# Seven-product MLP of a two-layer encoder: tiles on multiples of 512 bytes, and both layers' ends in another order

## The chip, the cores and the metric

The kernel runs on one core of a Trainium2 chip. The metric is device time in microseconds; runs of the kernel before gave 1194.27, 1194.92 and 1196.45 us, median 1194.92. Engines of a core: TensorE (PE, with its weight loads, PEld), VectorE (DVE), ScalarE (ACT), GpSimd (POOL) and SyncE (SP, whose queue issues most transfers). Each runs its own instructions in order; semaphores tie them together.

## What is computed

Two layers of an encoder on x of 512 tokens by 1024, everything in float32: attention (half stick-breaking heads, half differential heads) with an output projection, then an MLP with squared ReLU, each behind an RMSNorm and added to x, and one RMSNorm at the end.

```python
for l in range(DEPTH):                                   # DEPTH = 2
    h = rmsnorm(x, attn_norm[l])
    proj = jnp.einsum('bsd,de->bse', h, w_in[l])         # 1024 -> 3072
    ...
    x = x + jnp.einsum('bse,ed->bsd', mixed, w_o[l])
    h = rmsnorm(x, mlp_norm[l])
    u = jnp.square(jax.nn.relu(jnp.einsum('bsd,df->bsf', h, w_ff1[l])))   # D_FF = 4096
    x = x + jnp.einsum('bsf,fd->bsd', u, w_ff2[l])
return rmsnorm(x, final_norm)
```

## The kernel before

**Numbers.** Every fp32 operand of a large product is held as two parts: hi, a rounded copy made by ACT (L116 for weights, L223 for u), and lo, the rest, made by DVE (L117, L224). A product is three matmuls, hi with hi, hi with lo, lo with hi (`three`, L280 to L282), each 128 x 128 by 512 columns. The hi and lo parts of a weight unit (128 x 1024) take turns in four slots in the MLP: two in pool `wspl`, which lives through the whole kernel, and two in pool `f2`, opened for each layer's MLP. In attention only the first two are used.

**State.** x is kept transposed: eight tiles of 128 features by 512 tokens. h is x times the norm's gain, in hi and lo. The RMS factor of the MLP's input is not multiplied into h; since relu squared is homogeneous of degree two, its square (r2, one column for each 128 tokens, `column(tb)`) scales the output of the MLP.

**Attention.** `dense` yields the projections, matmul block by matmul block; `attn` yields the pieces of the heads' work. A loop interleaves them: for each cost of dense work, `credit` grows by cost * (ATT - spent) / (DENSE - TAIL - done), and attention pieces are issued while credit lasts. ATT = 54, DENSE = 145, TAIL = 6. What is left of attention at the end of dense follows in one go. In layer 1 the first two projection blocks (16 units of three matmuls) have already run at the end of layer 0 (`opened_by`).

**MLP.** Four groups of 1024 hidden features. Each has eight up-projection blocks (f, 24 matmuls each: weights stationary, h moving, L280 to L282). `evict_u` makes u in tile F (relu and square on ACT) and from it the sums and differences for a seven-product scheme (after Strassen) over halves of tokens and halves of features, split into Ah and Al. Then come seven forms in the order of FORMS, 24 matmuls each: Ah or Al stationary, the weight slot moving.

```python
FORMS = ("11", "21", "x1", "22", "x2", "x3", "x4")
```

The weight operands of forms 11, 21 and 22 are loaded as they are (`fetch`, SP's queue); those of x1, x2, x4 and x3 arise in place from accumulating transfers on POOL's queue (`grow`, L788). Products gather in seven tiles y (two banks of 128 tokens by 512 features each, `gather`, L838 to L840).

**Ends of the layers.** In the last group, the seven sums are combined to the four quarters of the output: `merge` (L848) adds one y to another by an accumulating transfer on POOL's queue, `join` (L845) does it on DVE. `settle` scales by column(tb): on ACT (L866), or on DVE as a scalar_tensor_tensor out of PSUM (L857). Layer 0 then transposes back into x (`back`: four transposes yT on PE, L871, an add on DVE, L872, and a new h), and starts the next layer's first projections, p. Layer 1 instead transposes x (xT, L862, inside `settle`) and adds it to y (L863), squares on ACT with a running sum (L881), `root` takes the power -1/2 on POOL (L886 to L889), `weigh` multiplies by the final gains, which lie in cos_t and sin_t (L893), and `store` scales and sends a half row out (L900 to L904). Banks for xT and yT have the tag "t", of which there are two.

**What sets the order.** Within an engine, the order is that of the program as the build's scheduler lays it out; PE, DVE, ACT and the queues of POOL and SP each hold to it. A tile's address follows from the order and sizes of tiles in the pools: cp (x, h, constants, up to the filler `trail`), wraw, wspl, and then the pool fp of the layer with y, kept (q), r2, F, Ah, Al and, in layer 1, four tiles `sum`; last comes f2.

## Time and profile before

| | |
|---|---|
| median of three runs | 1194.92 us |
| the profiled execution's own time | 1193.42 us |
| its span, first to last instruction | 1191.7 us |
| mean granted TensorE clock | 0.996 |
| layer 0: attention up to about 260, MLP about 260 to 580 us | |
| layer 1: attention about 580 to 860, MLP about 860 to 1181, end of the layer to 1191.7 | |

The profile is one execution. A row of a group reads: line, engine, operation, tile written <- tiles read, shapes, count | busy time, mean duration of one | idle time ahead of it on its engine, with what released it. A row in order of time reads: start, duration (of all merged ones together), engine, line, operation, tiles, count, and in brackets the idle time just before it and who ended it. Names of tiles come without their numbers; y tiles of the x forms are merged as yx, those of 11, 21 and 22 as y, and the PSUM banks of forms are 21030 (form 21, layer 0, group 3, bank 0) or x. Matmul rows overlap, so the distance from one start to the next is the measure of PE's pace.

### The profile page before, as it was taken

The numbers are of one execution on the slowest core, as the hardware profiler recorded it, in microseconds if no ns is written. First come the engines' busy times: TensorE is split into PE (matmuls) and PEld (weight loads), VectorE is DVE, ScalarE is ACT, GpSimd is POOL, SyncE is SP. The second block draws the span as 40 slices with busy tenths as digits, with TensorE's granted clock in tenths as the row PEclk, the third lists the DMA queues.
The fourth block names the chain that finished last, engine by engine and source line by source line (L and its number), as shares of the span: only waits on it lengthen the run. The fifth ranks groups of instructions, "written<-read, shape, count | busy, mean of one in ns | idle before, by whom it ended". The sixth has DMA issues, their size and how long they took to land.

```text
span 1191.7 us, 15321 instructions
## 1 busy us (share of the span) xinstructions
PE 1161.9 (98%) x5454; PEld 952.5 (80%) x5454; DVE 820.7 (69%) x1307; ACT 650.7 (55%) x1147; POOL 216.3 (18%) x281
## 2 busy tenths in 40 slices
PE   9999999999999999999999899999999999999995
PEld 6887888888888888888777788888888888888884
DVE  7888788765546646555978777887764466575668
ACT  6455666566655455455535455665665553653643
POOL 1221543120101001001011225332110010010021
PEclk9999999999999999999999999999999999999999
DMA  7545334254835837637326544432558367375273
GB/s 241 171 137 168 125 106 124 72 212 115 221 124 122 219 102 155 199 90 157 89 87 173 137 153 124 132 98 71 218 126 216 112 134 219 89 175 178 36 157 109
DMA packets 56716, 169.58 MB, mean 142 GB/s; under 512 B 7104, under 2 KB 8128, under 8 KB 56640
## 3 DMA queue, kind: packets, MB, share of 16 engines
q1 hardware_dynamic: 46416, 131.88, 33.7%
q0 software_dynamic: 10080, 36.70, 17.6%
q8 instruction: 43, 0.70, 0.2%
q14 instruction: 33, 0.27, 0.1%
q10 hardware_dynamic: 144, 0.02, 0.0%
HBM read 138.17 MB, written 2.10 MB: 118 GB/s over the span
## 4 chain that ended last, share of the span: by engine, by line
PE 80%; DVE 6%; DMA 4%; issue 4%; ACT 2%; POOL 2%; SPq 0%; POOLq 0%; DVEq 0%; ACTq 0%
PE f L281 10%; PE f L280 10%; PE f L282 10%; PE x L280 4%; PE x L281 4%; PE x L282 4%; DMA q<-in_w 2%; PE wo L280 2%; PE wo L281 2%; PE wo L282 2%; DVE wlo L117 1%; ACT whi L116 1%; PE T0s L554 1%; PE T1s L554 1%; DMA kl1d2k<-hl1d2k 1%
## 5 line engine op out<-in xcount | busy, mean ns | idle before, releaser
L117 DVE TENSOR_TENSOR wlo<-raw,whi 128x1024 fp32r<-128x1024 f32 (+1 forms) x132 | 158.9, 1207 | 105.0 <-ACT whi L116 104.3
L117 DVE TENSOR_TENSOR wlo<-q,whi 128x512 fp32r<-128x512 f32 x224 | 146.0, 686 | 98.1 <-ACT whi L116 98.0
L281 PE MATMUL f<-h_lo,whi 128*128 128x512 f32 x512 | 201.4, 393 | 0.0
L116 ACT ACTIVATE whi<-raw 128x1024 fp32r<-128x1024 f32 (+1 forms) x132 | 133.9, 1020 | 123.4 <-PE f L281 60.3
L280 PE MATMUL f<-h_hi,whi 128*128 128x512 f32 x512 | 201.0, 393 | 0.0
L282 PE MATMUL f<-h_hi,wlo 128*128 128x512 f32 x512 | 200.6, 392 | 0.0
L116 ACT ACTIVATE whi<-q 128x512 fp32r<-128x512 f32 x224 | 129.8, 625 | 127.3 <-PE f L281 38.0
L788 POOL DMA_DIRECT2D q<-in_w x64 | 55.9, 877 | 570.1 <-DVE wlo L117 493.4
L280 PEld LDWEIGHTS f<-h_hi,whi 128*128 128x128 f32 x512 | 96.1, 188 | 22.1
L282 PEld LDWEIGHTS f<-h_hi,wlo 128*128 128x128 f32 x512 | 96.1, 188 | 21.7
L281 PEld LDWEIGHTS f<-h_lo,whi 128*128 128x128 f32 x512 | 96.1, 188 | 21.5
L224 DVE TENSOR_TENSOR Al<-F,Ah 128x256 fp32r<-128x256 f32 (+2 forms) x96 | 74.8, 779 | 44.7 <-ACT Ah L223 44.7
L280 PE MATMUL x<-whi,Ah 128*128 128x512 f32 x256 | 101.8, 398 | 0.0
L281 PE MATMUL x<-wlo,Ah 128*128 128x512 f32 x256 | 101.4, 396 | 0.0
L282 PE MATMUL x<-whi,Al 128*128 128x512 f32 x256 | 101.1, 395 | 0.0
L223 ACT ACTIVATE Ah<-F 128x256 fp32r<-128x256 f32 (+2 forms) x96 | 67.6, 704 | 45.0 <-DVE F L824 43.0
L282 PEld LDWEIGHTS x<-whi,Al 128*128 128x128 f32 x256 | 48.4, 189 | 11.3
L280 PEld LDWEIGHTS x<-whi,Ah 128*128 128x128 f32 x256 | 48.4, 189 | 11.2
L281 PEld LDWEIGHTS x<-wlo,Ah 128*128 128x128 f32 x256 | 48.4, 189 | 11.0
L815 ACT ACTIVATE F<-f 128x512 f32<-128x512 f32 x64 | 37.6, 588 | 8.1 <-PE f L282 4.4
L816 ACT ACTIVATE F<-F 128x512 f32<-128x512 f32 x64 | 40.3, 630 | 1.5
L485 POOL TENSOR_TENSOR sig1s<-sig1s,C1s 128x128 f32<-128x128 f32 (+3 forms) x32 | 25.9, 809 | 61.9 <-DVE C1s L482 30.7
(1051 smaller groups left out, 2572.7 us busy)
## 6 DMA issues: line engine op xcount, KB each, us to landing
raw<-in_w SPq DMA_DIRECT2D x126, 512.0 KB, 3.5
q<-in_w SPq DMA_DIRECT2D x64, 512.0 KB, 5.5
q<-in_w POOLq DMA_DIRECT2D x64, 512.0 KB, 5.6
x<-in_xT SPq DMA_DIRECT2D x8, 256.0 KB, 4.3
raw<-in_w SPq DMA_DIRECT2D x8, 128.0 KB, 4.3
yx<-y POOLq DMA_DIRECT2D x2, 512.0 KB, 7.4
y<-y POOLq DMA_DIRECT2D x2, 512.0 KB, 8.1
y<-yx POOLq DMA_DIRECT2D x2, 512.0 KB, 6.2
```

Source lines behind the costliest of these rows:

```text
L116: h = nc.scalar.activation(hi[:, a:b], raw[:, a:b], AF.Copy)
L117: self.last = h, nc.vector.tensor_tensor(out=lo[:, a:b], in0=raw[:, a:b], in1=hi[:, a:b].bitcast(F32), op=ALU.subtract)
L223: nc.scalar.activation(hi, src, AF.Copy)
L224: nc.vector.tensor_tensor(out=lo, in0=src, in1=hi.bitcast(F32), op=ALU.subtract)
L280: nc.tensor.matmul(pt, ah, bh, start=first, stop=False)
L281: nc.tensor.matmul(pt, ah, bl, start=False, stop=False)
L282: nc.tensor.matmul(pt, al, bh, start=False, stop=last)
L485: nc.gpsimd.tensor_mul(sig[:, 0:wd], sig[:, 0:wd], C[:, 1 : wd + 1])
L554: nc.tensor.transpose(pt[:, off : off + P], u["w"][qi][:, kb * P : (kb + 1) * P], ident)
L788: nc.gpsimd.dma_start(t, quad(g, q, c), accum_op=ALU.add)
L815: nc.scalar.activation(t, pt, AF.Relu)
L816: nc.scalar.activation(t, t, AF.Square)
```

## The change

1. r2 and the sums leave fp: a tile `fin` of 24 columns in cp holds them, taken out of the filler `trail`, so that no other address in cp changes. What stands behind them in fp and f2 moves: F, Ah, Al and both f2 slots start on multiples of 512 bytes.
2. In layer 1, `done` starts at 2 * KC * 3 * 0.216 = 10.37, the cost of the two projection blocks that layer 0 has run.
3. The loads of cos_t and sin_t are issued in group 1 of the MLP; in layer 1, ACT scales both by the square root of D in group 2 (sin_t with a minus), and `weigh` and `root` lose those factors.
4. In the last group, merge 21 <- 11 follows gather 21 in place of gather 11.
5. Layer 0's end: y's rows are scaled by r2 on ACT beforehand, where they are complete, and products from PSUM or from x3 are multiplied and added (`add_to`). The join x4 <- x3 goes. Transposes back start after six of eight products of x4, in pairs, and the next layer's first products go in the order of c. All squares stand behind the last h.
6. Layer 1's end: for tokens 0 to 255, the second half gathers in "z", two quads' tiles that start as minus the transposed x (ACT) and get x1 times r2 by a transfer; two joins go; rows 2 and 3 are settled, squared and weighed within x3, and stored in the middle of x4.

```diff
     clo = cp.tile([P, 4], F32, tag="clo", name="clo")
     ones_r = cp.tile([P, 1], F32R, tag="onesr", name="ones_r")
     nc.vector.memset(ones_r.bitcast(F32), 1.0)
-    cp.tile([P, 112], F32, tag="trail", name="trail")
+    fin = cp.tile([P, 24], F32, tag="fin", name="fin")
+    cp.tile([P, 88], F32, tag="trail", name="trail")
 
...
             at = attn()
-            done = spent = credit = 0.0
+            done = 2 * KC * 3 * 0.216 if l else 0.0
+            spent = credit = 0.0
             live = True
...
             y = {f: fp.tile([P, 2, 512], F32, tag="y" + f, name=f"y{f}_{l}") for f in FORMS}
-            if not last:
-                nc.sync.dma_start(cos_t, cos)
-                nc.sync.dma_start(sin_t, sin)
-            else:
-                nc.sync.dma_start(cos_t, gfin[0:512].partition_broadcast(P))
-                nc.sync.dma_start(sin_t, gfin[512:1024].partition_broadcast(P))
-
             def quad(g, q, c):
...
             fresh = set(FORMS)
-            home = {(1, 0): "21", (1, 1): "22", (0, 0): "x4", (0, 1): "x1"}
+            home = {(1, 0): "21", (1, 1): "22", (0, 0): "x4", (0, 1): "z" if last else "x1"}
 
...
 
-            def settle(tb, j, banks_=None):
+            def turned(tb, j):
+                pt = bank("t", f"xT{tb}{j}")
+                for k in range(4):
+                    nc.tensor.transpose(pt[:, k * P : (k + 1) * P], x[:, 4 * j + k, tb * P : (tb + 1) * P], ident)
+                return pt
+
+            def settle(tb, j):
                 o = place(tb, j)
-                if banks_:
+                if last:
                     nc.vector.scalar_tensor_tensor(
-                        out=o, in0=banks_[tb % 2], scalar=column(tb), in1=o, op0=ALU.mult, op1=ALU.add)
-                elif last:
-                    pt = bank("t", f"xT{tb}{j}")
-                    for k in range(4):
-                        nc.tensor.transpose(pt[:, k * P : (k + 1) * P], x[:, 4 * j + k, tb * P : (tb + 1) * P], ident)
-                    nc.vector.scalar_tensor_tensor(
-                        out=o, in0=o, scalar=column(tb), in1=pt, op0=ALU.mult, op1=ALU.subtract if j else ALU.add)
+                        out=o, in0=o, scalar=column(tb), in1=turned(tb, j), op0=ALU.mult,
+                        op1=ALU.subtract if j else ALU.add)
                 else:
                     nc.scalar.activation(o, o, AF.Copy, scale=column(tb))
+
+            def add_to(tb, j, src):
+                o = place(tb, j)
+                nc.vector.scalar_tensor_tensor(
+                    out=o, in0=src, scalar=column(tb), in1=o, op0=ALU.mult, op1=ALU.add)
 
...
 
-            sums = {}
-
             def square(tb, j):
-                if tb not in sums:
-                    sums[tb] = fp.tile([P, 4], F32, tag=f"sum{tb}", name=f"sum{tb}")
                 nc.scalar.activation(
-                    ft(f"junk{tb}{j}"), place(tb, j), AF.Square, accum_out=sums[tb][:, j : j + 1])
+                    ft(f"junk{tb}{j}"), place(tb, j), AF.Square, accum_out=fin[:, 4 * tb + 4 + j : 4 * tb + 5 + j])
 
             def root(tb):
-                m = sums[tb]
-                nc.vector.tensor_tensor(out=m[:, 2:3], in0=m[:, 0:1], in1=m[:, 1:2], op=ALU.add)
-                nc.vector.tensor_scalar(
-                    out=m[:, 2:3], in0=m[:, 2:3], scalar1=1.0 / D, scalar2=EPS, op0=ALU.mult, op1=ALU.add)
-                nc.gpsimd.tensor_tensor(out=m[:, 3:4], in0=m[:, 2:3], in1=mhalf[:, 0:1], op=ALU.pow)
+                m = [fin[:, 4 * tb + 4 + n : 4 * tb + 5 + n] for n in range(4)]
+                nc.vector.tensor_scalar(out=m[2], in0=m[0], scalar1=m[1], scalar2=D * EPS, op0=ALU.add, op1=ALU.add)
+                nc.gpsimd.tensor_tensor(out=m[3], in0=m[2], in1=mhalf[:, 0:1], op=ALU.pow)
 
             def weigh(tb, j):
                 o = place(tb, j)
-                nc.vector.scalar_tensor_tensor(
-                    out=o, in0=o, scalar=-1.0 if j else 1.0, in1=(cos_t, sin_t)[j], op0=ALU.mult, op1=ALU.mult)
+                nc.vector.tensor_mul(o, o, (cos_t, sin_t)[j])
 
             def store(tb, j, weighed):
                 o = place(tb, j)
-                r = sums[tb][:, 3:4]
+                r = fin[:, 4 * tb + 7 : 4 * tb + 8]
                 if weighed:
...
 
-            r2 = fp.tile([P, 4], F32, tag="r2", name=f"r2{l}")
+            r2 = fin[:, 0:4]
             for g in range(GROUPS):
                 forms = {}
+                end = g == GROUPS - 1
+                if g == 1:
+                    if not last:
+                        nc.sync.dma_start(cos_t, cos)
+                        nc.sync.dma_start(sin_t, sin)
+                    else:
+                        nc.sync.dma_start(cos_t, gfin[0:512].partition_broadcast(P))
+                        nc.sync.dma_start(sin_t, gfin[512:1024].partition_broadcast(P))
+                if g == 2 and last:
+                    nc.scalar.activation(cos_t, cos_t, AF.Copy, scale=math.sqrt(D))
+                    nc.scalar.activation(sin_t, sin_t, AF.Copy, scale=-math.sqrt(D))
                 for k in range(2 * GP):
...
                     evict_u(pt, g, k, forms)
-                end = g == GROUPS - 1
+                    if end and k in (2, 3):
+                        settle(k - 2, 0)
                 for f, form in enumerate(FORMS):
...
                               n == mine[0], n == mine[-1])
-                        if tail and n == len(work) // 2 - 1:
-                            if last:
-                                settle(0, 0, to)
-                                square(0, 0)
-                                root(0)
-                                store(0, 0, False)
-                                store(0, 1, True)
-                            else:
-                                for c_ in CAME[:4]:
-                                    back(c_)
+                        if end and last and form == "x3" and n == 3:
+                            join("22", "x2")
+                            for tb in (2, 3):
+                                settle(tb, 1)
+                                square(tb, 1)
+                                root(tb)
+                                weigh(tb, 0)
+                        if tail and last and n == 3:
+                            add_to(0, 0, to[0])
+                            square(0, 0)
+                            weigh(2, 1)
+                            weigh(3, 1)
+                            root(0)
+                            for tb in (2, 3):
+                                for j in range(2):
+                                    store(tb, j, True)
+                        if tail and not last and n == 5:
+                            for c_ in CAME[:2]:
+                                back(c_)
                     if tail:
                         break
-                    if end and form == "x3":
+                    if end and not last and form == "x3":
                         for tb in (0, 1):
-                            settle(tb, 1, to)
+                            add_to(tb, 1, to[tb])
                     gather(form, to)
...
                         merge("x2", "11")
+                    elif form == "21":
                         merge("21", "11")
...
                             settle(tb, 0)
-                    elif form == "x2":
-                        join("x3", "x2")
-                        join("x1", "x3")
-                        join("22", "x2")
-                        for tb in (0, 1, 2, 3):
-                            settle(tb, 1)
                         if last:
                             for tb in (2, 3):
                                 square(tb, 0)
-                                square(tb, 1)
-                                root(tb)
+                            y["z"], t = (e.rearrange("p (a t) -> p a t", a=2) for e in kept[2])
+                            for tb in (0, 1):
+                                nc.scalar.activation(place(tb, 1), turned(tb, 1), AF.Copy, scale=-1.0)
+                                nc.scalar.activation(t[:, tb, :], y["x1"][:, tb, :], AF.Copy, scale=column(tb))
+                            y["t"] = t
+                            merge("z", "t")
+                    elif form == "x2":
+                        join("x3", "x2")
+                        if not last:
+                            join("x1", "x3")
+                            join("22", "x2")
+                            for tb in range(4):
+                                settle(tb, 1)
                     elif form == "x3":
-                        join("x4", "x3")
-                        for tb in (0, 1):
-                            settle(tb, 0)
                         if last:
                             for tb in (0, 1):
+                                add_to(tb, 1, y["x3"][:, tb, :])
                                 square(tb, 1)
-                                weigh(tb, 1)
-                            for tb in (2, 3):
-                                for j in range(2):
-                                    weigh(tb, j)
-                                    store(tb, j, True)
+                        for tb in (0, 1):
+                            add_to(tb, 0, y["x3"][:, tb, :])
             if last:
-                settle(1, 0, to)
+                add_to(1, 0, to[1])
                 square(1, 0)
+                store(0, 0, False)
+                weigh(0, 1)
+                store(0, 1, True)
+                weigh(1, 1)
                 root(1)
...
                 for tb in (0, 1):
-                    settle(tb, 0, to)
-                squares = []
-                for n, c in enumerate(CAME[:4]):
-                    squares.append(add_sq(c, n == 0, ft, nc.vector))
-                for i in range(2):
-                    for n, c in enumerate(CAME[:4]):
-                        three(pts[i], wpair(us[i], c), hpair(c), n == 0, False)
-                        if i == 1 and n in (1, 3):
-                            for c_ in CAME[4:6] if n == 1 else CAME[6:]:
-                                h = back(c_)
-                for c in CAME[4:]:
+                    add_to(tb, 0, to[tb])
+                for c in CAME[2:4]:
+                    back(c)
+                for n, c in enumerate(CAME):
+                    if n in (2, 3):
+                        for c_ in (CAME[4:6], CAME[6:])[n - 2]:
+                            h = back(c_)
                     for i in range(2):
-                        three(pts[i], wpair(us[i], c), hpair(c), False, c == CAME[-1])
-                for c in CAME[4:]:
-                    squares.append(add_sq(c, False, ft, nc.vector))
-                behind(squares[4][0], h[0])
-                behind(squares[4][1], h[1])
+                        three(pts[i], wpair(us[i], c), hpair(c), n == 0, c == CAME[-1])
+                squares = [add_sq(c, n == 0, ft, nc.vector) for n, c in enumerate(CAME)]
+                for n in (0, 1):
+                    behind(squares[n][n], h[n])
+                for p, q in zip(squares[1:], squares):
+                    behind(p[0], q[0])
                 opened_by.append(pts)
 
 
```

## The prediction

> **What bounds the kernel now.** I read the page first: busy shares, the engines of the chain that ended last, and the two dearest kinds of matmul.
>
> ```profile
> PE 1161.9 (98%) x5454; PEld 952.5 (80%) x5454; DVE 820.7 (69%) x1307; ACT 650.7 (55%) x1147; POOL 216.3 (18%) x281
> ...
> PE 80%; DVE 6%; DMA 4%; issue 4%; ACT 2%; POOL 2%; SPq 0%; POOLq 0%; DVEq 0%; ACTq 0%
> ...
> L280 PE MATMUL f<-h_hi,whi 128*128 128x512 f32 x512 | 201.0, 393 | 0.0
> ...
> L280 PE MATMUL x<-whi,Ah 128*128 128x512 f32 x256 | 101.8, 398 | 0.0
> ```
>
> PE is busy for 98% of the 1191.7 us span. A matmul row lasts 393 to 398 ns, but rows overlap, so what counts is how far apart matmuls start. The view of busy time by stretches then shows where PE has no air at all (columns: stretch, length, PE, PEld, DVE, ACT, POOL, granted clock, DMA share, GB/s).
>
> ```profile
> 270.00:500.00 230.00, 230.00 (x999) 187.42 (x999) 135.41 (x200) 124.00 (x193) 21.07 (x24) 1.00 0.61 158
> ...
> 570.00:600.00 30.00, 27.20 (x126) 21.80 (x125) 28.62 (x41) 17.87 (x28) 1.01 (x3) 0.94 0.28 72
> 600.00:870.00 270.00, 261.49 (x1337) 217.43 (x1336) 211.33 (x346) 148.22 (x290) 74.94 (x98) 1.00 0.44 135
> 870.00:1100.00 230.00, 230.00 (x994) 186.25 (x993) 132.77 (x193) 121.20 (x189) 20.90 (x24) 1.00 0.60 156
> ...
> 1165.00:1191.70 26.70, 12.89 (x63) 10.01 (x61) 21.45 (x38) 9.65 (x21) 4.35 (x4) 0.89 0.30 98
> ```
>
> In the MLP stretches (270 to 500, 870 to 1100) PE is busy 230.00 of 230.00 us while DVE has 59% and ACT 54%: there only the matmul's own interval counts. In the last 26.7 us it is the reverse, DVE has 21.45 and PE 12.89. Layer 1's attention (600 to 870) loses 8.5 us of PE.
>
> Last I read the order of time on PE, at the first matmul of each block of 24.
>
> ```profile
> 338.15 0.40 PE L280 MATMUL f<-h_hi,whi 128*128 128x512 f32 x1
> ...
> 343.75 0.39 PE L280 MATMUL f<-h_hi,whi 128*128 128x512 f32 x1
> ...
> 349.22 0.39 PE L280 MATMUL f<-h_hi,whi 128*128 128x512 f32 x1
> ...
> 553.67 0.39 PE L280 MATMUL x<-whi,Ah 128*128 128x512 f32 x1
> ...
> 559.13 0.40 PE L280 MATMUL 22030_5103<-whi,Ah 128*128 128x512 f32 x1
> ...
> 564.73 0.39 PE L280 MATMUL x<-whi,Ah 128*128 128x512 f32 x1
> ...
> 907.07 0.40 PE L280 MATMUL x<-whi,Ah 128*128 128x512 f32 x1
> ...
> 912.67 0.39 PE L280 MATMUL x<-whi,Ah 128*128 128x512 f32 x1
> ```
>
> Blocks of the same 24 matmuls come in two lengths, with no idle in either. In the up-projection 338.15 to 343.75 is 5.60 us, and 343.75 to 349.22 is 5.47. In layer 0's products, x1 takes 5.46 (553.67 to 559.13) and 22 takes 5.60; in layer 1, x2 takes 5.60. Divided by 24: 233.3 or 227.7 ns a matmul.
>
> **The change part by part.**
>
> *Placement.* In the built program before, r2 (16 bytes, in a 32-byte step) pushes F, Ah and Al to 32 past a multiple of 512, and the two weight slots of pool f2 to 32 (layer 0) or, behind the four sums, 160 (layer 1). h, the other two weight slots and all y lie on multiples. Sorted by these addresses, the long blocks are those whose two operands differ modulo 512: up-projections out of an f2 slot, products out of the other slots, and in layer 1 all products (32 against 160 or 0). Short ones have 0 with 0, or 32 with 32. Afterwards every pair is 0 with 0, which the up-projection at 343.75 already has. Blocks that shorten: layer 0 half of 32 up-blocks and half of 28 products, layer 1 half of 32 and all 28: 16 + 14 + 16 + 28 = 74. Each gives 5.60 - 5.46 = 0.14 us. The last two lie under a DVE bound, so 72 x 0.14 = 10.1 us, all on the path, since PE has no idle to absorb it. Bounds: 0, if something else of these slots (who fills them, when) makes the difference, and 11. I take 10.1, as the same two slots are fast with Ah and slow with h in layer 0, which rules out the slot itself.
>
> [...]
>
> *Layer 0's end and its merges.* y's merge 21<-11 goes on POOL's queue behind the next quad's accumulation.
>
> ```profile
> 554.20 0.88 POOL L848 DMA_DIRECT2D y<-y  x1 [1.59 <-issue]
> 556.92 0.88 POOL L788 DMA_DIRECT2D q<-in_w  x1 [1.84 <-issue]
> ...
> 562.59 0.69 DVE L840 TENSOR_TENSOR y<-y,21030_5021 128x512 f32<-128x512 f32 x1 [6.76 <-DMA y<-y]
> ...
> 563.31 1.34 ACT L866 ACTIVATE y<-y,r 128x512 f32<-128x512 f32 x2 [5.54 <-DVE y L840]
> 565.00 3.24 ACT L116 ACTIVATE whi<-q 128x512 fp32r<-128x512 f32 x6 [0.35 <-PE 22031_5104 L282]
> ...
> 567.48 0.39 PE L280 MATMUL x<-whi,Ah 128*128 128x512 f32 x1
> ...
> 574.91 1.22 DVE L845 TENSOR_TENSOR yx<-yx,yx 128x1024 f32<-128x1024 f32 x1
> ...
> 580.05 1.40 DVE L857 SCALAR_TENSOR_TENSOR yx<-x,r,yx 128x512 f32<-128x512 f32 x2
> ...
> 580.85 0.33 PE L871 MATMUL yT<-edge,yx 128*128 128x128 f32 x1 [2.14 <-DVE yx L857]
> ```
>
> The 6.76 us that gather 21 waits for its merge disappear from DVE, and the quad comes up to 2.7 us earlier (556.92 - 554.20). The merge itself is issued up to 2.7 us later and so lands near 565; ACT's scaling of y21 (563.31), which waits for it, holds the splits of 565.00 by about 1.4 us. PE takes up that quad at 567.48, 2.5 after that row, so 22 and half of x2 cover it; uncovered it would be 1.4 us of PE. At the end one join goes (1.14 from start to start, row 574.91) and two scalar_tensor_tensor (STT, 0.66 to 0.70 each) come, so the last two STT end up to 0.9 later than the 581.45 of the row at 580.05. The stall of 2.14 ahead of the first yT is covered by six more matmuls of x4 (1.4) to about 1.0 to 1.6; what is late next is the second pair of yT, whose banks wait for DVE's x+=yT behind those STT and a weight split: about 2 us. The p products then run in order of c instead of i, so PE has work between the transposes, but all squares now stand behind the last split of h, and the first projection that needs their sum may lose 0.8 more. Sum 0, bounds 2.5 lost and 2 gained, the first being this second stall uncovered, the second the old one gone.
>
> *Layer 1's pacing.* done starts at 10.37 instead of 0, so attention is issued at 54/128.6 instead of 54/139 per unit of dense work, 8% faster; nothing is computed less.
>
> ```profile
> 631.20 0.35 PE L464 MATMUL S1d<-st1d0k,st1d0q 128*128 128x256 f32 x1 [0.84 <-DMA st1d0q<-hl1d0k]
> ...
> 661.95 0.36 PE L464 MATMUL S1d<-st1d2k,st1d2q 128*128 128x256 f32 x1 [3.21 <-DMA kl1d2k<-hl1d2k]
> 662.14 0.39 PE L282 MATMUL p1d3q<-h_hi,wlo 128*128 128x512 f32 x1
> ```
>
> The long idles are scores that wait for their rotated heads by DMA. Issued earlier they wait longer by as much, behind them in PE's queue stand the p1d3 products, and the stage ends earlier by what was left over. 0, with 2 either way (the 3.21 halved or made half as long again, rounded up).
>
> *Layer 1's end.*
>
> ```profile
> 1157.40 3.24 ACT L116 ACTIVATE whi<-q 128x512 fp32r<-128x512 f32 x6 [7.18 <-PE 22131_10247 L282]
> ...
> 1162.01 1.40 DVE L863 SCALAR_TENSOR_TENSOR y<-y,r,xT 128x512 f32<-128x512 f32 x2
> ...
> 1166.94 1.27 DVE L840 TENSOR_TENSOR yx<-yx,x 128x512 f32<-128x512 f32 x2
> ...
> 1168.74 1.21 DVE L845 TENSOR_TENSOR yx<-yx,yx 128x1024 f32<-128x1024 f32 x1
> ...
> 1173.54 0.66 PE L862 MATMUL xT<-edge,x 128*128 128x128 f32 x4 [3.23 <-DVE yx L863]
> 1173.95 0.47 PE L280 MATMUL x<-whi,Ah 128*128 128x512 f32 x1
> ...
> 1181.81 1.28 DVE L893 SCALAR_TENSOR_TENSOR y<-y,sin_t 128x512 f32<-128x512 f32 x2
> ...
> 1184.55 0.16 DVE L886 TENSOR_TENSOR sum<-sum 128x1 f32<-128x1 f32 x1
> ...
> 1187.23 0.75 DVE L902 SCALAR_TENSOR_TENSOR yx<-yx,sum,cos_t 128x512 f32<-128x512 f32 x1 [0.67 <-POOL sum L889]
> ```
>
> From gather x2 (1166.94) to the last STT (1187.98) DVE runs 21.0 us nearly without a hole, then 3.7 us of output transfer follow to 1191.7. The new list behind gather x2 at the same row prices: gathers x2 and x3 2.4, two halves of wlo 1.2, two joins (of four) 2.3, two settles 1.3, six add_to 4.0, four weighs 2.4, three or four tiny sums 0.3, two stores 1.3: 15.2, plus 0.7 waiting for one root, 15.9. That saves 5.1. New on PE: xT01 now stands after only three matmuls of x2, with two banks of its kind, and waits for the first STT of row 1162.01 (about 1160.5 to 1161.1 with the merge's new place). PE, free at 1157.4, is there near 1158.8, so it stands 2.3 us, with all of x2 queued behind. x2 then ends at 1157.4 + 16 transposes (0.41 for four, 1173.54 to 1173.95) 1.7 + 24 matmuls 5.5 + 2.3 = 1166.9, which is when DVE comes to it anyway (1166.94). New ACT copies and z's merge (a POOL transfer of 512 KB) lie under x2 and x3. The loads of cos_t and sin_t move from ahead of the stage to g = 1 on SP's queue, behind quads that are fetched a group ahead, and nobody waits for them before the end. The two scalings of cos_t and sin_t at g = 2 lie in ACT's 46% idle; uncovered they would be 1.3 us.
>
> *The clock.* A new stall can cost a second time.
>
> ```profile
> 583.39 0.63 PE L281 MATMUL x<-wlo,Ah 128*128 128x512 f32 x1
> ...
> 585.09 0.39 PE L282 MATMUL x<-whi,Al 128*128 128x512 f32 x1
> ```
>
> After the 2.14 of idle at 580.85 matmuls lasted 0.63 until 585, at a mean granted clock of 0.94 over 30 us: 1.7 us lost. After the 3.21 at 661.95 the next lasted 0.39, none lost. So a stall of 2 to 3 us draws this about every second time: 0.8 off the 5.1, and I take 4.0 for the end (bounds 1, with the stall, a dip and z late; 6, without the stall). [...]
>
> **Sum.** 10.1 + 0 + 0 + 4.0 = 14.1. The profiled execution took 1193.4, so its like takes 1179.3; it lies 1.5 under the median of 1194.9, which gives 1180.8, say 1181.
>
> **The rivals.**
> *Offsets don't matter* (8%). Then only the end pays: 1194.9 - 4.0 = 1191. For it: the address is only what the two lengths go by, not shown to cause them. Against: three different pairs sort the same way.
> *Placement pays, the ends don't* (14%). Each new in-order wait costs its bound: 10.1 gained, 2.5 lost at layer 0, the end 1 gained less a further dip of 1.7: about 1187. For it: PE is told to transpose before DVE is ready, twice.
> *Everything pays* (11%): 10.1, 6 at the end, boundary 2, half of the pacing's bound: 1176.
> *DVE becomes layer 1's attention bound: slower* (7%). DVE is at 211.33 of 270 there, 78%, locally more. Issued 8% faster, each of the 24 attention units could find its inputs unready and stall PE as at 631.20: 24 x 0.84 = 20 us, less 14.1: 1201. It decides from about 0.6 us a unit on. Against: 8% on 78% is 84%, still under 1.
>
> **How the numbers follow.** My forecast has 60%, with 1177 to 1185 as its own range. A measurement of this kernel can tell 0.2% (2.4 us) from no change. Faster: 60 + 14 + 11 and half of the first rival's 8 (its 1191 lies close to the bound), 89%; same 4%; slower 7%. The range goes from 1174 (everything pays) to 1190 (the ends don't pay, bounds added), leaving out the first and last rival and some of the third.
>
> **What would show it.** Every block of 24 at 5.45 to 5.47 us in both layers, and f and x rows a few ns shorter: placement right; 5.60 anywhere: wrong. The first DVE idle for y21's merge gone, and PE idle near yT of some 1 and 2 us instead of 2.14 once: boundary right. A PE idle of about 2.3 us at xT01, released by DVE, and last DVE work about 16 us behind gather x2: end right. The same two score idles in layer 1's attention, of like size: pacing right. I am wrong if PE in the MLP stretches shows idle (the splits or quads no longer keep up), or if the attention of layer 1 loses clearly more than 8.5 us.

## The result and the profile after

| | before | after |
|---|---|---|
| median (runs) | 1194.32 us (6) | 1172.99 us (6, 1172.03 to 1176.53) |
| profiled execution, own time | 1193.42 us | 1172.68 us |
| its span | 1191.7 us | 1170.9 us |

The ratio is 0.9822, with a 95% interval of 0.9809 to 0.9836: 21 us less, where 14 were forecast. The time lies 1 us under the range. A later set of runs of the changed kernel, on another occasion, gave 1174.34 (four runs, 1172.73 to 1175.23) against 1194.24.

The page of the changed kernel, same lines as before (line numbers in the new file are 1 higher here):

```profile
PE 1147.6 (98%) x5454; PEld 951.2 (81%) x5454; DVE 813.1 (69%) x1302; ACT 651.5 (56%) x1153; POOL 212.7 (18%) x282
...
PE 86%; DVE 5%; DMA 2%; issue 2%; ACT 1%; POOL 0%; SPq 0%; POOLq 0%; DVEq 0%; ACTq 0%
...
L281 PE MATMUL f<-h_hi,whi 128*128 128x512 f32 x512 | 199.6, 390 | 0.0
...
L281 PE MATMUL x<-whi,Ah 128*128 128x512 f32 x256 | 100.0, 391 | 0.0
```

PE does the same 5454 matmuls in 14.3 us less. Rows of f fell from 393 to 390 ns, of x from 398 to 391. The busy time by stretches, columns as before:

```profile
268.00:498.00 230.00, 230.00 (x1016) 190.44 (x1015) 137.50 (x201) 126.16 (x198) 21.12 (x24) 1.00 0.61 161
...
565.00:596.00 31.00, 27.07 (x132) 21.22 (x130) 29.47 (x44) 16.07 (x26) 1.01 (x3) 1.00 0.29 68
596.00:829.00 233.00, 228.59 (x1198) 191.99 (x1199) 187.00 (x320) 130.11 (x267) 69.78 (x97) 1.00 0.42 127
829.00:1059.00 230.00, 230.00 (x1018) 190.43 (x1017) 134.42 (x197) 128.81 (x201) 22.91 (x25) 1.00 0.61 165
...
1140.00:1170.90 30.90, 20.11 (x100) 16.26 (x98) 24.34 (x40) 16.12 (x35) 4.80 (x7) 0.94 0.53 135
```

230 us of the MLP now hold 1016 and 1018 matmul rows, where they held 999 and 994: PE is still never idle there, it is faster. The view in order of time on PE shows how much, at first matmuls of blocks of 24:

```profile
331.05 0.39 PE L281 MATMUL f<-h_hi,whi 128*128 128x512 f32 x1
...
336.49 0.39 PE L281 MATMUL f<-h_hi,whi 128*128 128x512 f32 x1
...
341.93 0.39 PE L281 MATMUL f<-h_hi,whi 128*128 128x512 f32 x1
...
548.65 0.39 PE L281 MATMUL x<-whi,Ah 128*128 128x512 f32 x1
...
554.09 0.39 PE L281 MATMUL 22030_5105<-whi,Ah 128*128 128x512 f32 x1
...
559.53 0.39 PE L281 MATMUL x<-whi,Ah 128*128 128x512 f32 x1
```

Each of these blocks takes 5.44 us, 226.7 ns a matmul, up-blocks and forms x1 and 22 alike, and so do nearly all others of both MLPs.

To see where 20.8 us of span went, both profiled executions are cut at the same five instructions on PE: layer 0's last x4, the first v projection of layer 1 (p1w0v), layer 1's first up-block (at 839.6 before, so attention ends there and not at about 860), the transposes xT20 that follow form 22 of the last group, and the end.

| stage | before | after | less | forecast |
|---|---|---|---|---|
| up to layer 0's last x4 | 575.8 | 570.8 | 5.0 | 4.2 (30 blocks x 0.14) |
| x4 to p1w0v: layer 0's end | 25.7 | 25.1 | 0.5 | 0 |
| p1w0v to the first up-block: layer 1's attention | 238.2 | 233.2 | 4.9 | 0 |
| up-block to xT20: layer 1's MLP | 317.6 | 311.6 | 6.1 | 5.9 (42 blocks) |
| xT20 to the end | 34.4 | 30.2 | 4.2 | 4.0 |

Four of five stages came within 1 us of the forecast. The third did not.

### The profile page after: what moved, and what is told of

Its sections match the earlier page's. It is cut to its first block, busy times and chain, and to the rows that moved or that the text cites. A ratio compares the mean times of both kernels' runs of the same rounds, so it can differ in the third digit from the quotient of the medians.

```text
span 1170.9 us, 15335 instructions
## 1 busy us (share of the span) xinstructions
PE 1147.6 (98%) x5454; PEld 951.2 (81%) x5454; DVE 813.1 (69%) x1302; ACT 651.5 (56%) x1153; POOL 212.7 (18%) x282
## 4 chain that ended last, share of the span: by engine, by line
PE 86%; DVE 5%; DMA 2%; issue 2%; ACT 1%; POOL 0%; SPq 0%; POOLq 0%; DVEq 0%; ACTq 0%
PE f L283 10%; PE f L281 10%; PE f L282 10%; PE x L281 4%; PE x L283 4%; PE x L282 4%; PE wo L281 3%; PE wo L283 3%; PE wo L282 3%; DMA q<-in_w 2%; DVE wlo L117 1%; PE T1s L555 1%; PE T0s L555 1%; PE O0s L584 0%; PE O1s L584 0%
## 5 line engine op out<-in xcount | busy, mean ns | idle before, releaser
L228 ACT ACTIVATE h_hi<-x,g_all 128x512 fp32r<-128x512 f32 x32 | 22.5, 718 | 26.6 <-DVE x L692 13.8
```

Source lines behind the costliest of these rows:

```text
L228: a = nc.scalar.activation(h_hi[:, c, :], x[:, c, :], AF.Copy, scale=g)
```

## Experiments

Each kernel was run beside the kernel before on the same chip. Stage lengths below are those of one profiled execution each, cut as in the table above: start to x4 / layer 0's end / attention / layer 1's MLP / end. Half clock (in the kernel before 3.41 us from 581.66 on at a granted clock of 0.50, with matmul rows of 0.63 us in place of 0.39) comes in some executions and not in others; by an estimate from that clock, it moves a stage by 1.7 us for each 3.4 us of it.

| kernel | median, us | ratio, 95% | stages, us |
|---|---|---|---|
| placement alone | 1183.73 | 0.9913 (0.9894, 0.9932) | 570.5 / 25.6 / 239.8 / 310.9 / 35.1 |
| pacing alone | 1189.05 | 0.9955 (0.9938, 0.9971) | 576.1 / 25.3 / 233.0 / 317.2 / 35.5 |
| ends and merges alone | 1192.81 | 0.9983 (0.9969, 0.9998) | 577.0 / 26.2 / 241.0 / 318.5 / 29.5 |
| all but pacing | 1178.72 | 0.9872 (0.9847, 0.9896) | 570.9 / 26.8 / 236.8 / 311.9 / 30.1 |
| all, every tile 32 further | 1175.45 | 0.9837 (0.9808, 0.9866) | 572.1 / 25.1 / 233.2 / 311.5 / 32.5 |
| all, F to f2 64 further | 1186.71 (one run) | | 576.9 / 26.4 / 233.1 / 316.6 / 31.9 |
| all, F to f2 128 further | 1181.67 (one run) | | 575.0 / 26.1 / 233.3 / 316.2 / 29.3 |
| all, F to f2 256 further | 1178.61 (one run) | | 570.7 / 26.7 / 233.8 / 312.4 / 33.3 |
| all, half the head start | 1179.68 | 0.9851 (0.9818, 0.9883) | 573.0 / 26.6 / 238.0 / 311.5 / 32.5 |
| all, twice the head start | 1179.25 | 0.9875 (0.9842, 0.9907) | 569.8 / 26.1 / 238.9 / 311.5 / 30.9 |
| all, xT01 and xT11 later | 1176.38 | 0.9828 (0.9800, 0.9856) | 572.0 / 26.5 / 233.5 / 311.5 / 31.4 |
| all, merge 21 <- 11 in its old place | 1180.96 | 0.9871 (0.9846, 0.9896) | 571.4 / 26.4 / 233.8 / 311.5 / 37.2 |
| before, one load behind head d2 | 1189.89 | 0.9968 (0.9956, 0.9981) | 575.9 / 25.3 / 234.7 / 317.6 / 35.6 |
| all, one load behind head d3 | 1177.79 | 0.9855 (0.9830, 0.9879) | 570.2 / 26.4 / 235.8 / 311.5 / 34.1 |
| all, once more | 1174.34 | 0.9826 (0.9807, 0.9845) | 571.5 / 26.5 / 233.8 / 311.5 / 30.0 |

### The change taken apart

Placement alone, in the kernel before:

```diff
-    cp.tile([P, 112], F32, tag="trail", name="trail")
+    fin = cp.tile([P, 24], F32, tag="fin", name="fin")
+    cp.tile([P, 88], F32, tag="trail", name="trail")
...
-                    sums[tb] = fp.tile([P, 4], F32, tag=f"sum{tb}", name=f"sum{tb}")
+                    sums[tb] = fin[:, 4 * tb + 4 : 4 * tb + 8]
...
-            r2 = fp.tile([P, 4], F32, tag="r2", name=f"r2{l}")
+            r2 = fin[:, 0:4]
```

> The kernel before with r2 and the sums moved to cp, nothing else. Theory A (what counts is that the two operands of a matmul start at the same offset modulo 512): all blocks of 24 in the MLP take 5.44 to 5.46 us, layer 0's MLP gets 5 us and layer 1's 6 us shorter, and the whole about 11 us: 1183. Theory B (the MLP got faster in the changed kernel because weights come earlier, by merges, pacing and ends): blocks stay at 5.60, the time stays at 1194.

Measured 1183.73 against 1195.22. Both MLPs shortened as in the changed kernel, attention and both ends did not. Theory A: moving 80 bytes of small tiles is worth 11 us.

Pacing alone, in the kernel before:

```diff
-            done = spent = credit = 0.0
+            done = 2 * KC * 3 * 0.216 if l else 0.0
+            spent = credit = 0.0
```

> The kernel before with layer 1's attention paced faster, nothing else. Theory A (pacing made the 4.9 us that layer 1's attention got shorter): from the first v projection (p1w0v) to the first up-block of layer 1 it takes 233 us in place of 238, and the whole is 4 to 5 us faster, 1189.5. Theory B (that stage got faster because of what layer 0's end leaves behind, weight splits and squares in another order): 238 stays, and the time is 1194 within 1.

Measured 1189.05, attention 233.0 us. Theory A: the gain of that stage is the pacing's, with nothing else of the change there.

Ends and merges alone: the changed kernel with r2 and the sums as tiles of fp again and with done starting at 0.

> The changed kernel with addresses and pacing of before: only merges and both ends are new. Theory A (ends are worth what the two traces show at their places, 0.5 at layer 0's end and 4.2 at layer 1's): 1189.5, and layer 1's attention stays at 238 us. Theory B (the order at layer 0's end is what shortens attention): about 1185, attention 233 to 234.

Measured 1192.81. Layer 1's end takes 29.5 us, so it gained 5; layer 0's end did not gain, and attention stayed long (241.0). Theory B is out; A held for layer 1's end, but the whole is 3 us worse than it said. In the profile there are a wait of 0.84 in x2 of the last group of layer 0, and two stretches of half clock, 3.4 us ahead of attention and 6.8 us in it.

All but pacing: the changed kernel with done starting at 0.

> The changed kernel with layer 1's attention paced as before. Theory A: attention goes back to 238 us, with a wait of 3 us for kl1d2k and a late remainder, 1178. Theory B (the gain comes from the rest): 1173 within 1.

Measured 1178.72, the time of theory A. Its stage is only near: attention takes 236.8 us, not 238, and the wait at the third head is 1.63, not 3. Differences of the medians: placement 11.5, pacing 6.2 alone (95%: 3.5 to 7.4) and 5.7 inside the change (taken over two occasions), ends 2.4.

### What the operands' offsets must satisfy

All tiles 32 bytes further (the first filler of cp grows from 96 to 104 columns), so that nothing lies on a multiple of 512 and all operands agree:

> The changed kernel with the first filler of cp 32 bytes longer, so that every tile of the kernel starts at 32 past a multiple of 512 and the operands of each matmul still agree with each other. Theory A (agreement of the two operands decides): all MLP blocks of 24 stay at 5.44 to 5.47 us, 1173 within 1. Theory B (multiples of 512 themselves decide): all blocks at 5.60, MLPs 11 to 19 us longer, 1185 to 1192.

1175.45, an up-block at 5.44 us (330.87 to 336.31), and both MLPs at the changed kernel's length but for one wait of 1.06 us at 563.29; the rest of what it is above theory A's 1173 lies in its end (32.5 us). Agreement decides, not the multiple. Then three pads ahead of F (`fp.tile([P, n // 4], F32, tag="pad", ...)` before r2's line), n = 64, 256 and 128:

> The changed kernel with a pad of 64 bytes ahead of F, so that F, Ah, Al and both f2 slots start at 64 past a multiple of 512, the rest on multiples. Theory A (offsets must agree modulo 512): half of the up-blocks and half of the products take 5.60 us again, as in layer 0 before, about 9 us longer, 1182. Theory C (they must agree only modulo 64): every block at 5.45, 1173.

> The same with a pad of 256 bytes. Theory A (modulo 512): the same half of the blocks at 5.60 us, 1182. Theory C (modulo 256 or a part of it): every block at 5.45 us, 1173.

> The changed kernel with a pad of 128 bytes ahead of F. Offsets that differ by 256 cost nothing and by 64 cost 6.5 ns a matmul. Theory A (offsets must agree modulo 256): half of the blocks at 5.60 us, about 1184. Theory B (modulo 128): all at 5.44, 1173 to 1177.

The same stretch of the up-projection of layer 0, group 1, in the order of time on PE: first two blocks out of f2 slots and then the first out of the others. With 64:

```profile
333.04 0.39 PE L281 MATMUL f<-h_hi,whi 128*128 128x512 f32 x1
...
338.64 0.39 PE L281 MATMUL f<-h_hi,whi 128*128 128x512 f32 x1
...
344.24 0.40 PE L281 MATMUL f<-h_hi,whi 128*128 128x512 f32 x1
```

With 128:

```profile
332.08 0.40 PE L281 MATMUL f<-h_hi,whi 128*128 128x512 f32 x1
...
337.69 0.40 PE L281 MATMUL f<-h_hi,whi 128*128 128x512 f32 x1
...
343.29 0.40 PE L281 MATMUL f<-h_hi,whi 128*128 128x512 f32 x1
```

With 256:

```profile
331.20 0.39 PE L281 MATMUL f<-h_hi,whi 128*128 128x512 f32 x1
...
336.64 0.39 PE L281 MATMUL f<-h_hi,whi 128*128 128x512 f32 x1
...
342.08 0.39 PE L281 MATMUL f<-h_hi,whi 128*128 128x512 f32 x1
```

With 64 and 128 the blocks with unequal operands take 5.60 us, with 256 all take 5.44. So the forecast's "modulo 512" is too strict: modulo 256 is what these runs show. That the run with 256 took 1178.6 lies for about half in its end (33.3 us against 30.2, with a stall of 4.09 at xT01 and half clock behind it) and for 1.5 us in layer 0's end; its MLPs give 0.8. The run with 64 (1186.7) is slower than the 1182 of theory A, with both MLPs 5 to 6 us longer than in the changed kernel.

### What pacing does

The stretch of attention before, with the pacing alone, and with one edit that comes below:

```profile
601.00:839.00 238.00, 229.66 (x1197) 191.75 (x1197) 189.05 (x317) 127.49 (x262) 72.24 (x96) 1.00 0.42 122
```

```profile
601.00:834.00 233.00, 228.63 (x1198) 191.84 (x1198) 185.89 (x318) 128.50 (x264) 69.59 (x97) 1.00 0.44 127
```

```profile
601.00:836.00 235.00, 230.13 (x1199) 192.30 (x1200) 189.73 (x317) 127.23 (x262) 72.22 (x96) 1.00 0.42 125
```

The same matmuls in 238, 233 and 235 us. Cut at the first stick-breaking projection (p1s0q), the gain has two parts: 77.4 to 74.6 us ahead of it and 160.8 to 158.5 behind it. The cut does not part the same work: with the pacing six matmuls O1d of 0.12 us run ahead of it that stood behind it before. Corrected by these 0.7 us, 3.6 us were gained ahead of the cut and 1.6 behind it. Ahead of it all is idle time of PE (6.57 to 3.00 us); behind it idle fell only from 1.76 to 1.37, and the rest is that matmuls start closer together. To this second part belongs the remainder: before, attention was not done when the dense work of wo(1) ended; its last pieces ran between 812.94 and 818.87, with wo(0)'s first products scattered among them:

```profile
812.94 0.40 PE L282 MATMUL wo<-mdh,wlo 128*128 128x512 f32 x1
813.17 0.28 PE L582 MATMUL O1s<-zh,vs 128*128 128x256 f32 x1
...
818.75 0.28 PE L583 MATMUL O1s<-zl,vs 128*128 128x256 f32 x1
818.87 0.40 PE L282 MATMUL wo<-vdh,wlo 128*128 128x512 f32 x1
```

In the changed kernel attention ends at 804.8, with twelve matmuls of wo(1) still to come. Two other doses:

> The changed kernel with half the head start (5.2 in place of 10.4) for layer 1's attention. Theory A (two thresholds: the wait at the third differential head goes with any shift of its work, the remainder behind the last wo1 product goes only when attention ends ahead of it): part of the gain, 1174 to 1177, a shorter remainder between wo1 and wo0. Theory B (the head start that was chosen is just past the best, as twice of it cost 6 us): 1171 to 1172.

> The changed kernel with twice the head start for layer 1's attention (done starts at 20.7 in place of 10.4). Theory A (the gain is one removed wait at the third differential head and a remainder at the end that is gone already): no further gain, 1172 to 1175, the stage from p1w0v to the first up-block at 233 us or a little above. Theory B (each 8% of pace is worth 5 us): 1168, the stage at 228. Theory C (attention now outruns its inputs): slower, above 1176, with new waits of the scores for DMA.

Half the head start gave 1179.68, no clear gain over none (1178.72): both theories missed, and A's two thresholds came the other way round. The remainder ended (158.5 us behind p1s0q, as with all of it), but not the wait ahead of it: 79.5 us there, with 3.4 us of half clock at that wait. The first score of that head on PE:

```profile
660.08 0.55 PE L465 MATMUL S1d<-st1d2k,st1d2q 128*128 128x256 f32 x1 [2.48 <-ACT p1d L522]
```

and how long the transfers of kl1d2k took, from the view of that tile:

```profile
DMA to landing us min/median/max: 4.7/5.2/5.5
```

The row names ACT, but the score starts 0.2 us after the third transfer of st1d2q has landed (659.85), as it does in the kernel before (661.75, score at 661.95).

Twice the head start lost 6 us: the time of theory C. There are two waits of scores of 2.1 us, where the changed kernel has one of 1.53, and 3.4 us of half clock at the first of them:

```profile
678.92 0.35 PE L465 MATMUL S1d<-st1d3k,st1d3q 128*128 128x256 f32 x1 [2.09 <-issue]
...
779.05 0.39 PE L466 MATMUL S1s<-kl1s3k,st1s3q 128*128 128x256 f32 x1 [2.10 <-DMA kl1s3k<-hl1s3q]
```

What removes the wait at the third differential head? Its transfers (kl1d2k and others, 128 KB each) took a median of 6.1 us to land before and 3.3 us with the pacing alone (medians of kl1d2k). SP's queue before, in order of time, and then the landing times of kl1d2k:

```profile
652.59 0.54 SPq L99 DMA_DIRECT2D raw<-in_w  x1
653.23 0.54 SPq L407 DMA_DIRECT2D st1d2q<-hl1d2k  x1
...
657.05 0.60 SPq L407 DMA_DIRECT2D st1d2q<-hl1d2k  x1
659.77 0.54 SPq L407 DMA_DIRECT2D kl1d2k<-hl1d2k  x1
```

```profile
DMA to landing us min/median/max: 3.7/6.1/6.8
```

A weight load of 512 KB goes out just ahead of the head's last eight transfers, and the last of these goes out only at 659.77. With the pacing alone that load goes out at 650.11, two of the head's transfers earlier in the queue. One edit in the kernel before sends it behind all of them:

```diff
     def load(self, n):
...
-            self.nc.sync.dma_start(t, self.dram[self.loaded])
+            d = self.nc.sync.dma_start(t, self.dram[self.loaded])
+            if self.lead:
+                self.lead(d)
...
                     ready[(kind, b)] = clock[0] + DLY_D
+                    if (l, b) == (1, 2):
+                        W.lead = lambda d: (behind(d, z), setattr(W, "lead", None))
```

(z is the head's last transfer; `behind` orders two instructions of one queue.)

> The kernel before with one edit in SP's queue: the 512 KB weight load that stands between the transfers of layer 1's third differential head goes behind all of them. Theory A (that load, not the pace itself, makes the head's last transfers land 6 us after their issue, and so the wait of 3.2 us): the transfers land in 3 to 4 us, the wait at 658 falls to 1 us or less, the stage from p1w0v to the first up-block takes 235 to 236 us in place of 238, and the time is 2 to 4 us lower. Theory B (the head is ready too late on DVE, whatever the queue holds): the wait stays within 0.5 us of 3.2, 1194 to 1196.

SP's queue, the landing times of kl1d2k and the head's first score on PE in that kernel:

```profile
652.69 0.54 SPq L410 DMA_DIRECT2D st1d2q<-hl1d2k  x1
...
657.15 0.60 SPq L410 DMA_DIRECT2D kl1d2k<-hl1d2k  x1
657.80 4.04 SPq L100 DMA_DIRECT2D raw<-in_w  x3
```

```profile
DMA to landing us min/median/max: 2.6/2.7/2.7
```

```profile
657.98 0.36 PE L469 MATMUL S1d<-st1d2k,st1d2q 128*128 128x256 f32 x1 [0.24 <-issue]
```

The transfers land in 2.7 us, all eight go out without a hole, and the wait, 3.21 us at 661.95 before, falls to 0.24. Attention takes 234.7 us, and the time fell by 0.32% (0.19 to 0.44), 3.8 us: theory A. The remainder is untouched (160.6 us behind p1s0q), as it must be. The load's place does not fix the size of the wait: with the same order in the queue it was 3.62 us in placement alone, 3.01 in ends and merges alone and 1.63 in all but pacing, where the transfers landed in 4.4 us. The same edit in the changed kernel, at the fourth head ((1, 3) in place of (1, 2)):

> The changed kernel with the same edit at the fourth differential head (the load at 670 behind the head's transfers). Theory A (the load delays the head): its wait of 1.5 us falls, about 1 us gained. Theory B (the head is late on DVE): 1.5 us stays, and the time is that of the changed kernel.

A miss of theory A. The transfers of that head land in 2.6 to 2.7 us, but they did so without the edit too (2.6 to 2.8), and the waits there are still 1.31 and 0.37 where one of 1.53 was. That agrees with theory B: DVE ends the head at 672.80 and 673.40, and its last eight transfers go out from 672.86 on, one each 0.6 us. The stage behind p1s0q took 160.9, 2.4 more, of which 3.4 us of half clock from 680.5 on make some 1.7, and the time is above the changed kernel's own of the same occasion, with intervals that overlap:

> The changed kernel itself once more, on the chip of these runs, to compare the others with: 1173 within 2 if the stalls seen in the other runs (1.1 us at x2 of layer 0, 1.6 to 4.1 at xT01) come by the execution and not by the edit; both stalls then vary here too.

1174.34. Its profile has a wait of 0.70 at x2 of layer 0 and one of 2.37 at xT01, so these come by the execution, in size at least.

### The ends

> The changed kernel with the transposes xT01 and xT11, and what follows from them, after twelve products of x2 instead of three and four. My forecast's step: the PE stall at xT01 (2.6 us in the changed kernel's profile) delays gather x2 by no more than DVE's own lateness. Theory A (x2's end sets gather x2): the stall goes, gather x2 starts 1 us earlier, 1172. Theory B (z's merge and ACT's copies come too late for x3's additions): 1174 to 1176, with DVE waiting for z's transfer.

(The lines that make z move from behind form 22 into form x2, at n == 3.) 1176.38: nothing gained. The stall moved with the transposes, 2.16 us, released by the same scalar_tensor_tensor on DVE, which came late here behind weight splits. Neither theory's number held, and the runs' scatter (1172.7 to 1177.2) is larger than the effect.

The merge back in its old place:

```diff
                     if form == "11":
                         merge("x2", "11")
-                    elif form == "21":
                         merge("21", "11")
                     elif form == "22":
```

> The changed kernel with merge 21 <- 11 issued next to the other merge of form 11, as before. Theory A (the moved merge is hidden at both ends): 1173 within 1, with DVE idle 6 to 7 us at gather 21 again. Theory B (gather 21's wait delays the chain of both ends): 1175 to 1177.

1180.96, worse than either theory. The new end needs the moved merge. In order of time on PE and on DVE in that kernel:

```profile
1152.83 1.11 PE L852 MATMUL xT<-edge,x 128*128 128x128 f32 x4 [6.76 <-DVE y L858]
```

```profile
1143.40 0.69 DVE L835 TENSOR_TENSOR y<-y,21130_10178 128x512 f32<-128x512 f32 x1 [8.94 <-DMA y<-y]
```

Gather 21 waits 8.94 us for its merge, everything behind it on DVE is late, and xT01, which stands early in x2 on PE, now waits 6.76 us for a bank instead of 2.61. The end takes 37.2 us, more than the old end's 34.4.

## Why the prediction was right in four steps and wrong in one

**Placement: right, sized too low.** 74 blocks gave 0.14 us each by forecast; they gave 0.16 (5.60 to 5.44), and the 46 others, 5.44 to 5.49 before, fell to 5.44 too. Against 10.1 forecast, placement alone took 12.0 us out of the two stages with the MLPs (5.3 and 6.7) and 11.5 by medians; in the changed kernel these stages give 11.1, with eight transposes more in layer 1's. The first rival, that offsets don't matter, fell with the first experiment. Where the two operands of a matmul start cost PE 6.7 ns in 233 here.

**Layer 0's end: right within its bounds.** 0 forecast, 0.5 gained in this execution, by luck: of the thirteen profiles with this end the two without half clock there took 25.1 us, the eleven with it 26.1 to 26.8, and the four with the old end 25.3 to 25.7, two of them with half clock. DVE's wait of 6.76 for y21's merge is gone as forecast. What the forecast called uncovered, the splits held on ACT behind that merge, came in four profiles (ends and merges alone, all tiles 32 further, half the head start, and the changed kernel once more): PE waits 0.70 to 1.06 us for ACT at x2. The second stall forecast at the yT pairs is there: 1.29 us and 1.88 us of idle, where before there was 2.14 once.

```profile
576.29 0.33 PE L872 MATMUL yT<-edge,yx 128*128 128x128 f32 x1 [1.29 <-DVE yx L866]
...
581.20 0.44 PE L872 MATMUL yT<-edge,yx 128*128 128x128 f32 x2 [1.88 <-DVE x L873]
```

**Pacing: wrong.** The step that failed reads "Issued earlier they wait longer by as much ... 0, with 2 either way". It took the wait of 3.21 us as one for work that is simply not ready, so that shifting both sides leaves it. It was a wait for transfers held up by one weight load ahead of them in SP's queue: moving that load alone took the wait to 0.24, 3.4 us out of the stage and 3.8 off the time. With the pacing the load goes out earlier (650.11 in place of 652.59), ahead of more of the head's transfers, these land in 3.3 us, and the wait is gone; that the load's earlier issue is all there is to it, no run shows. The chain of waits had named the DMA; what I did not read was SP's queue in order of time around it, where the load stands at 652.59. What lies behind p1s0q, with the remainder that the same step set aside as "what was left over", was worth 1.6 us. In the changed kernel a wait of 1.53 at the fourth head, 0.16 and 0.39 before, is the largest that is left:

```profile
677.53 0.35 PE L465 MATMUL S1d<-st1d3k,st1d3q 128*128 128x256 f32 x1 [1.53 <-DMA kl1d3k<-hl1d3k]
```

The stage gained 4.9 us where 0 was forecast. The medians say 5.7 to 6.2; half clock right behind the third head's wait, which three of the five profiles with that wait have (placement alone, ends and merges alone, half the head start), may be the difference, but that was not tested. Of the 6.6 us by which the stages' 20.7 exceed the 14.1 forecast, pacing is 4.9, placement 1.0 and the ends 0.7. With pacing's 4.9 alone the time would have been 1176, still inside the range; the sum of all put it 1 us under. The slower rival, DVE as the bound of a faster attention, did not come at this pace; with twice the head start 6 us are lost, 3.3 of them in more idle time of PE, and which engine sets these waits was not traced.

**Layer 1's end: right, its size in part by luck.** 4.0 forecast, 4.2 measured (4.9 against the kernel with placement alone). On PE and on DVE:

```profile
1145.02 0.66 PE L852 MATMUL xT<-edge,x 128*128 128x128 f32 x4 [2.61 <-DVE y L858]
```

```profile
1150.27 1.37 DVE L835 TENSOR_TENSOR yx<-yx,x 128x512 f32<-128x512 f32 x2
...
1166.37 0.75 DVE L896 SCALAR_TENSOR_TENSOR yx<-yx,fin,cos_t 128x512 f32<-128x512 f32 x1 [0.66 <-POOL fin L884]
```

The stall at xT01 was forecast at 2.3 us and is 2.61. From gather x2 to the end of the last row DVE needs 16.85 us, against 15.9 forecast and 21.0 before. So DVE saved 4.2, not 5.1, and the half clock that the forecast took off at 0.8 did not come in this execution: two errors that cancel. Without half clock at this place the new end took 29.3 to 30.2 us in five profiles, and the old one 34.4 in one; with it, 30.9 to 34.1 in six and 35.1 to 35.6 in three.

**The clock.** Half clock came and went as said: the changed kernel's profile has no such stretch ahead of its last matmul (granted clock 1.00 over 0 to 1162.7), most of the other profiles have one of 3.4 us just ahead of layer 1's attention or within it, and eleven have 3.4 or 6.8 us at layer 1's last transposes (7 or 8 tenths of the clock in the last of the 40 slices of their pages, where the others have 9). By the estimate above each 3.4 us costs some 1.7 us. What stood ahead of it in the kernel before is in the last section.

**Two slips of the sum.** The second rival's parts (10.1 gained, 2.5 lost, 1 gained, 1.7 lost) give 1188, not 1187, and the range's 1174 is called "everything pays", which the same text puts at 1176. The measured time lies below both.

## What to carry to other kernels

Look at where in memory the two operands of the matmuls that fill the critical path start: here a 16-byte tile allocated in front of large ones and, in layer 1, four more of that size cost 6.7 ns of each of some 1800 matmuls. When scores or any small transfers hold up an engine, read the queue that issues them in order of time: a large prefetch just ahead of them can be the cause, and one edit that moves it (3.8 us here) tells. An edit that moves one wait (the merge) may be what makes another edit (the early transposes) pay, so take them apart in both directions.

## What was not expected of the hardware

- Matmuls 128 x 128 by 512 of fp32r, back to back, start 226.7 ns apart (blocks of 5.44 us) when the start addresses of stationary and moving operand agree modulo 256, and 232.1 to 233.3 apart (5.57 to 5.60) when they differ by 32, 64, 128 or 160. Of equal offsets, 0 with 0, 32 with 32 and 0 with 256 were run. What in the chip does that, these runs do not show.
- The four 128 KB transfers kl1d2k behind a 512 KB one on the same queue landed in a median of 6.1 us after their issue in the kernel before, and in 4.4 us in all but pacing, which has the same order; ahead of it, in the kernel with that load moved, 2.7 us.
- How long PE stood idle does not tell by itself whether half clock follows. In the kernel before, 3.41 us of it (granted clock 0.50 from 581.66 to 585.07) came 0.81 us after the end of a wait of 2.14 us, with PE busy for 0.95 of the 3.42 us ahead of it. Up to the last matmul it is the only such stretch from 5 us on: the third head's wait of 3.21 us, with PE busy for 0.20 of the 3.41 us up to its end, drew none. Nor did the waits of 1.29 and 1.88 us at yT in the changed kernel (granted clock 1.00 over 565 to 596), whereas all but pacing, with the same end of layer 0, had 0.94 over 570 to 600. What decides it was not shown.
